# Three scan stages get their first part in the last convolution, and VectorE does the first and the last of the 15 steps of each inverse

## The chip, the cores and the metric

The kernel runs on one core of a Trainium2 chip. Its engines are named as the profile names them: PE (TensorE, matrix products), DVE (VectorE), ACT (ScalarE), POOL (GpSimd), and SP, whose queue issues nearly all of the transfers. Each works through its own instructions in order, and semaphores tie them together. The metric is the device time of one execution, in microseconds (us), as the median of several runs.

## What is computed

One layer of a hybrid model, on 128 context tokens and 2048 latent tokens of 1024 channels. Both token sets are normalised and modulated, go through one input projection, and then through two groups of heads: a delta-rule recurrence (RWKV-7) over 8 heads of 64 channels, run in both directions, and a short gated convolution. An output projection and a last norm follow.

```python
proj = h @ lp['w_in']
r, k, v, g_a, b_gate, c_gate, u_conv, g_b = jnp.split(proj, IN_SPLITS, axis=-1)
...
def step(S, inp):
    r_t, w_t, k_t, v_t, kk_t, a_t = inp
    s_kk = jnp.einsum('bdhij,bdhj->bdhi', S, kk_t)
    S = (S * w_t[..., None, :] - s_kk[..., :, None] * (kk_t * a_t)[..., None, :]
         + v_t[..., :, None] * k_t[..., None, :])
    return S, jnp.einsum('bdhij,bdhj->bdhi', S, r_t)
...
ya = ya.astype(x.dtype) * jax.nn.silu(g_a)
yb = b_gate * _short_conv(c_gate * u_conv, lp['conv_w'], is_latent) * jax.nn.silu(g_b)
u = jnp.concatenate([ya, yb], axis=-1) @ lp['w_out']
return x + gate * u, s_final
```

The recurrence isn't run token by token. The tokens are cut into chunks of 64. In a chunk the corrections of all tokens depend on each other through a triangular matrix of 64 x 64, whose inverse is needed; with it a chunk becomes a few products, and a chain of one small product (S) per chunk carries the state.

## The kernel before

**Three phases.** `phase1` projects the input in three thirds of the tokens. For each third it prepares the recurrence's operands (`recurrence`) and writes them to DRAM, then does the convolution of eight units (`groupB`, four channel groups of two token blocks each); each unit takes 96 matmuls and some DVE and ACT work. `phase2` is the scan: 17 stages, of 16 chunks each (two groups of eight, one per direction). `phase3` is the output projection, whose first parts are mixed into the last stages.

**One stage of the scan** (names as in `SEQ`; a digit at the end is the direction's group):

- *First part.* `L` loads the operands (`rr`). `Gm`, `Qm`, `Fm` are products and transposes on PE (L1019 and L1028); `Ge`, `Fe` (DVE, L1037), `Qe`, `Fa` (ACT) evict them into the stage's slot (`F`, `GA`, `Q`). `dg` (DVE, L1058) takes the diagonal blocks of 32 x 32, `ab` turns them (DVE, L1063), `zi` sets up the inverse `zt` (ACT), `pre` prepares pairs of columns (DVE, L1081 and L1082), and `I` (`inverse`, POOL) does 15 steps of three instructions each: a product into `ztmp` (L1091) and two differences into `zt` (L1094).
- *Second part.* `zr` and `zd` transpose the result (DVE, L1102 and L1105); `U`, `W` (PE), `bu`, `n`, `c0`, `c1` (ACT) join the 32 x 32 blocks to inverses of 64 x 64 in `zb`; `X` (PE, L1171) and `Xc` (ACT) solve; `E` (PE, L1189) and `Ev` (DVE, L1194) build each chunk's operator.
- *The chain.* `S` (PE, L1220) applies the operator to state and values, `sv` (DVE, L1246) scales the new state for the next chunk, `y` collects outputs, and `fw` to `fa` finish a block.

**Order.** `SEQ` is one body of the scan: `S20` is chunk 2 of direction 0 of this stage, `Ge0+3` an eviction of the stage three ahead, `y10+-1` an output of the stage before. So body b works on the chain of stage b, the operators and the inverse's ends of later stages (`I+2`, `zr+2`, `zd+2`, `U+2`), and the first part of stage b + 3. From body 0 on, PE, DVE and ACT keep that order exactly (`manual_schedule`, 13 bodies, then the list `LATE`, which also mixes in `phase3`). POOL, SP and everything ahead of body 0 are put in order by the compiler's own planner, which goes by priority and by which buffers are free; a tile's buffer is free when its last user in the program has run.

**The way in.** While the last third's convolution runs, `early` is stepped four times behind each of its eight units. It opens the right-hand pools of the scan and does the first parts of stages 0 and 1, into two slots in `O.r0`. `main` follows when `phase1` has closed its left-hand pools: `setup_rest` opens `O.l0`, `O.l1` (with `zb`, `zr`, `zd`) and `O.r2` (with the third slot), and the bodies -3 to -1 of `SEQ` fill the pipeline: among them the first part of stage 2 and the second part of stages 0 and 1. `ab` and `zt` have two buffers each, `dg` one.

**Memory.** In `phase1` the raw weight tiles `wr` (two of 4 KB a partition) are in the pool `wp`, beside the split weights `w`, which live to the end of the last convolution. The raw tiles are not used any more in the last third.

Of the kernel before, what the change touches and what calls it, by code (L numbers as in the profile page):

```python
# [6 lines left out]
F32 = mybir.dt.float32  # L7
# [3 lines left out]
ALU = mybir.AluOpType  # L11
# [51 lines left out]
def phase1(K):  # L63
    nc, tc, A, S = K.nc, K.tc, K.A, K.S
    V, G, P, T = nc.vector, nc.gpsimd, nc.scalar, nc.tensor
    cp = Pool(K, "p1c", "left")
    wp = Pool(K, "p1w", "left", 2)
    hl = Pool(K, "p1h", "left", 2)
    tp = Pool(K, "p1t", "left")
    ca = Pool(K, "p1ca", "right")  # L70
    hr = Pool(K, "p1hr", "right")
# [551 lines left out]
    def gate_rows():  # L623
        for b in range(2):
            pr = None
            for k2 in range(4):
                wt = wp.tile([128, 2, 512], F32, tag="wr", name=f"wgate{b}{k2}", bufs=2)
# [45 lines left out]
    for t3, js in enumerate(THIRD):  # L673
# [92 lines left out]
LATE = """  # L766
I@15 sv51@12 fa@10.1 Ge0@16 E110@13 Ev001@13 gh10@14 E010@13 Ev110@13 E100@13 gh00@14 Ev010@13 Gm1@16
# [12 lines left out]
S71@14 CH@4 E110@15 svL1@16 sv71@14 E100@15 CH@5 CD@4 fw@14.0 CD@5 WL@0 zr@16 WL@1 zd@16 U@16 fr@14.0 c1@16  # L780
y11@14 c0@16 Ev100@15 Ev110@15 E111@15 bu@16 E101@15 Ev111@15 WH@0 E000@15 Ev101@15 WH@1 E001@15 WD@0
# [34 lines left out]
def phase2(K):  # L816
# [4 lines left out]
    B = Ctx()  # L821
# [3 lines left out]
    def setup_first():  # L825
# [35 lines left out]
    def setup_rest():  # L861
# [4 lines left out]
        O.r2 = Pool(K, "p2r2", "right")  # L866
        new_slot(O.r2)
        cp = O.l0
# [215 lines left out]
    def inverse(name, s, st, gi):  # L1084

        ab, zt = st.ab, st.zt
        tmp = tl([128, 256], "ztmp", 1, O.rI)
        for m in range(15):
            j, kn, n = 2 * m, m + 1, 30 - 2 * m
# [3 lines left out]
            for r in range(2):  # L1093
                G.tensor_tensor(zt[:, :kn, j + 2:32], zt[:, :kn, j + 2:32], tv[:, :, r], ALU.subtract)  # L1094

    rows = [(slice(sl * 64, sl * 64 + 32), slice(sl * 64 + 32, sl * 64 + 64)) for sl in range(2)]

    def zrows(name, s, st, gi):

        if name == "zr":  # L1100
            st.zr = tl([128, 16, 32], "zr", 1, O.l1)
            V.transpose(st.zr[:].rearrange("p u (q h) -> p q h u", h=2), st.zt[:].rearrange("p q i -> p (q i)"))  # L1102
# [230 lines left out]
    def ending(name, s, st, gi):  # L1333
# [3 lines left out]
        if st.fin is not None:  # L1337
            next(st.fin, None)

    DO = dict(Gm=product, Qm=product, Fm=product, Ge=m_evict, Qe=m_evict, Fa=m_evict, Fe=m_evict, dg=diag, ab=turn, zi=begin, pre=pre, I=inverse,  # L1340
              zr=zrows, zd=zrows, c0=zcopies, c1=zcopies, U=merge, bu=merge, W=merge, n=merge, gh=gcopies, X=solve, Xc=solve,
              E=operator, Ev=operator, S=state, sv=scaled, y=outputs,
              fw=ending, fr=ending, fq=ending, fm=ending, T=ending, fy=ending, fa=ending)
    LOAD = dict(L=load_rr, gsL=load_gs, fsL=load_fs, svL=load_sv)
    SOLO = "ab zi pre I zr zd c0 c1 U bu W n fw fr fq fm T fy fa".split()

# [15 lines left out]
    def first(s):  # L1362
# [23 lines left out]
    def main():  # L1386
# [262 lines left out]
```

## Time and profile before

| what | us |
|---|---|
| median of three runs (1579.95 to 1585.35) | 1580.28 |
| span of the profiled execution, from its first to its last instruction | 1578.3 |
| PE busy | 1499.9 (95%) |
| DVE busy | 1139.9 (72%) |
| ACT busy | 772.3 (49%) |
| POOL busy | 573.8 (36%) |
| POOL, L1094 of the inverse (510 instructions) | 215.4 |
| POOL, L1091 of the inverse (255 instructions) | 139.4 |

The page gives no other time of the profiled execution than its span. The span is cut into places by rows of the timeline: the last third's convolution runs until 946.8 us, the way into the scan follows, the first transposes `zr` of a body are at 988.93 (body 0), 1011.12 (body 1) and so on to 1282.54 (body 12), and the last inverse's `zr` is at 1335.25. An idle time of an engine counts only where another engine waits for what it does next; the page's chain and the waits say where that is.

### The profile page before, as it was taken

What the parts mean: (1) busy time and instruction counts of PE and PEld (TensorE: products, weight loads), DVE (VectorE), ACT (ScalarE), POOL (GpSimd) and SP (SyncE); (2) the same over time, 40 slices, a digit from 0 to 9 for tenths busy, and PEclk for the clock granted to TensorE, in tenths of its full rate; (3) what the DMA queues carried; (4) which work ended last, traced back from release to release, by engine and by line L of the source; (5) the groups of instructions that cost most, each with busy time, mean ns of one, the idle gap of its engine ahead of it and who ended that gap; (6) DMA issues with size and microseconds to landing.
All of it is one profiled execution on the core that took longest, in us unless ns stands there. A gap on an engine that the chain in (4) does not pass through costs nothing.

```text
span 1578.3 us, 39371 instructions
## 1 busy us (share of the span) xinstructions
PE 1499.9 (95%) x16208; PEld 1381.2 (88%) x16208; DVE 1139.9 (72%) x1957; ACT 772.3 (49%) x1462; POOL 573.8 (36%) x962
## 2 busy tenths in 40 slices
PE   5999999999999999999999998999999998899998
PEld 2899999999999999899998997888888886678786
DVE  5999995764999735449985428798998997746533
ACT  4566652432555213135551107887878777523222
POOL 0133330001333100013322805888788887212221
PEclk7899999999999999999999998999999999999999
DMA  9669998663878865438887537566676754646442
GB/s 371 213 174 264 269 270 332 223 223 115 225 220 217 233 226 180 145 116 233 261 218 267 194 125 178 150 188 159 194 192 179 193 163 149 180 142 188 151 143 93
DMA packets 204579, 313.78 MB, mean 199 GB/s; under 512 B 58088, under 2 KB 147560, under 8 KB 190320
## 3 DMA queue, kind: packets, MB, share of 16 engines
q1 hardware_dynamic: 168816, 311.13, 63.9%
q10 hardware_dynamic: 35584, 0.14, 1.4%
q8 instruction: 127, 2.08, 0.6%
q14 instruction: 52, 0.43, 0.1%
HBM read 208.05 MB, written 103.17 MB: 197 GB/s over the span
## 4 chain that ended last, share of the span: by engine, by line
PE 65%; DVE 14%; POOL 7%; issue 5%; DMA 5%; ACT 2%; SPq 0%; ACTq 0%; DVEq 0%; POOLq 0%
POOL zt L1094 4%; PE psu L1503 4%; PE psu L1504 4%; PE psu L1505 4%; PE psE L1189 3%; POOL ztmp L1091 3%; PE mmb L182 2%; PE mmb L184 2%; PE mmb L183 2%; PE psS L1220 2%; PE mmc L182 2%; PE mmc L184 2%; PE mmc L183 2%; PE mmu L182 2%; PE mmu L184 2%
## 5 line engine op out<-in xcount | busy, mean ns | idle before, releaser
L1094 POOL TENSOR_TENSOR zt<-zt,ztmp 128x30 f32<-128x30 f32 (+7 forms) x510 | 215.4, 422 | 39.8
L1091 POOL TENSOR_TENSOR ztmp<-ab,zt 128x60 f32<-128x60 f32 (+7 forms) x255 | 139.4, 547 | 66.7 <-DVE ab L1082 47.0
L410 POOL TENSOR_TENSOR sh<-rawl 128x384 f32<-128x384 f32 (+1 forms) x48 | 47.5, 1007 | 210.1 <-ACT rawl L401 210.1
L1220 PE MATMUL psS<-sv,E 128*64 128x64 f32 x2176 | 104.6, 229 | 12.8 <-DVE sv L1246 7.3
L1220 PEld LDWEIGHTS psS<-sv,E 128*64 128x64 f32 x2176 | 82.8, 137 | 37.9 <-issue 16.3
L1194 DVE TENSOR_TENSOR E<-psE,msk 128x512 f32<-128x512 f32 x136 | 90.6, 683 | 20.0 <-PE psE L1189 18.9
L1568 POOL TENSOR_TENSOR z<-z,x 128x512 f32<-128x512 f32 x32 | 42.7, 1337 | 147.6 <-DVE z L1562 85.7
L1175 ACT ACTIVATE stf<-psX 64x512 f32<-64x512 f32 x136 | 80.3, 590 | 13.1 <-PE psX L1171 10.7
L434 POOL TENSOR_TENSOR hsl<-sq,hsh 128x384 fp32r<-128x384 f32 (+1 forms) x24 | 34.1, 1421 | 129.9 <-ACT hsh L429 121.6
L1246 DVE TENSOR_TENSOR sv<-psS,pc 64x128 f32<-64x128 f32 x254 | 63.7, 271 | 22.4 <-PE psS L1220 21.7
L182 PE MATMUL mmg<-h,w 128*128 128x384 f32 (+1 forms) x216 | 70.8, 328 | 0.0
L183 PE MATMUL mmg<-h,w 128*128 128x384 f32 (+1 forms) x216 | 70.7, 327 | 0.0
L184 PE MATMUL mmg<-h,w 128*128 128x384 f32 (+1 forms) x216 | 70.7, 327 | 0.0
L219 POOL TENSOR_TENSOR hslq<-ssq,hshq 128x384 fp32r<-128x384 f32 (+1 forms) x4 | 4.8, 1202 | 174.2 <-ACT hshq L218 109.6
L182 PE MATMUL mmb<-h,w 128*128 128x384 f32 (+1 forms) x192 | 63.9, 333 | 4.0 <-DMA w<-scr_wsp 4.0
L182 PE MATMUL mmv<-h,w 128*128 128x384 f32 (+1 forms) x192 | 63.1, 329 | 0.9 <-DVE sg L524 0.6
L184 PE MATMUL mmc<-h,w 128*128 128x384 f32 (+1 forms) x192 | 62.8, 327 | 1.0 <-DVE w L154 1.0
L184 PE MATMUL mmb<-h,w 128*128 128x384 f32 (+1 forms) x192 | 63.7, 332 | 0.0
L183 PE MATMUL mmb<-h,w 128*128 128x384 f32 (+1 forms) x192 | 63.6, 331 | 0.0
L182 PE MATMUL mmu<-h,w 128*128 128x384 f32 (+1 forms) x192 | 63.0, 328 | 0.2
L182 PE MATMUL mmc<-h,w 128*128 128x384 f32 (+1 forms) x192 | 63.0, 328 | 0.0
L184 PE MATMUL mmu<-h,w 128*128 128x384 f32 (+1 forms) x192 | 62.9, 328 | 0.0
(312 smaller groups left out, 5019.6 us busy)
## 6 DMA issues: line engine op xcount, KB each, us to landing
w<-scr_wsp SPq DMA_DIRECT2D x68, 1024.0 KB, 5.4
scr_wsp<-w SPq DMA_DIRECT2D x34, 1024.0 KB, 6.0
rr<-scr_ops SPq DMA_DIRECT2D x32, 1024.0 KB, 6.7
scr_ops<-xs SPq DMA_DIRECT2D x160, 192.0 KB, 6.5
wr<-in_win SPq DMA_DIRECT2D x34, 512.0 KB, 8.2
x<-in_x SPq DMA_DIRECT2D x17, 512.0 KB, 3.9
wadas<-in_wada SPq DMA_DIRECT2D x8, 1024.0 KB, 13.9
sv<-scr_vt SPq DMA_DIRECT2D x32, 256.0 KB, 4.0
```

Of the source, the lines that this page charges most:

```text
L182: T.matmul(ps[:, :n], w[:, 0, k], hh[:, 0, k, :n], start=k == 0, stop=False)
L183: T.matmul(ps[:, :n], w[:, 0, k], hh[:, 1, k, :n], start=False, stop=False)
L184: T.matmul(ps[:, :n], w[:, 1, k], hh[:, 0, k, :n], start=False, stop=k == 7)
L1091: G.tensor_tensor(tv, ab[:, j:j + 2, j + 2:32].unsqueeze(1).broadcast_to((128, kn, 2, n)), zt[:, :kn, j:j + 2].unsqueeze(3).broadcast_to(( ...
L1094: G.tensor_tensor(zt[:, :kn, j + 2:32], zt[:, :kn, j + 2:32], tv[:, :, r], ALU.subtract)
L1175: P.activation(g.fs[64:128, :, hd, e::2], g.ps["X"][e][hr_].rearrange("p a (b t) -> p b a t", b=2), AF.Copy, scale=-1.0)
L1194: V.tensor_tensor(g.E[n][:, k:k + 2].rearrange("p a b c -> p (a b) c"), pe[:].rearrange("p a b c -> p (a b) c"), B.msk[:, ME[g.d]].unsquee ...
L1220: T.matmul(g.sp[i // 4][r, q, hd, :], g.E[n][:, k, hd, r], g.sv[:, u, hd, :], start=True, stop=True)
L1246: V.tensor_tensor(dst, g.sp[i // 4][0:64, q], B.pc[0:64, d, 2 * p:2 * p + 2, c:c + 1].broadcast_to((64, 2, 64)), ALU.mult)
L1503: T.matmul(ps[:], mh[:, n], hi[:, cs], start=start and n == 0, stop=False)
L1504: T.matmul(ps[:], mh[:, n], lo[:, cs], start=False, stop=False)
L1505: T.matmul(ps[:], ml[:, n], hi[:, cs], start=False, stop=stop and n == 3)
```

## The change

Four edits. First, `early` does the first part of three stages in place of two; the third slot moves from `O.r2` to a pool of its own, `O.r3`, that is opened with the others. Second, to make room for it, the raw weight tiles of `phase1` get a pool of their own, `wrp`, closed when the last third's convolution begins. Third, the inverse on POOL does steps 1 to 13 only. Step 0 becomes `zf` (`first_row`, two DVE instructions behind `pre`), with `dg` as its scratch tile. Step 14 becomes `zl` (`last_columns`, three DVE instructions ahead of `zr`), with the tile of `zr` as its scratch. Fourth, `zf` and `zl` are put into `SEQ`, `LATE` and `first`. Numbers of buffers stay as they were.

```diff
+    wrp = Pool(K, "p1r", "left")
...
-        raw = wp.tile([128, 8, 128], F32, tag="wr", name=f"wr{cb}_{K.u()}", bufs=2)
+        raw = wrp.tile([128, 8, 128], F32, tag="wr", name=f"wr{cb}_{K.u()}", bufs=2)
...
-            for p in (pax, ta_, hr, ca):
+            for p in (pax, wrp, ta_, hr, ca):
...
-S21 L0+4 Fa0+3 Qe0+3 zi+3 sv30 S40 Fe0+3 fm sv21 sv40 Fm1+3 L1+4 X0+1 S50 pre+3 T sv50 Fa1+3 Fe1+3 S31
-S60 sv31 fy Xc00+1 init+1 y00 Xc10+1 X1+1 S41 Xc01+1 sv60 S70 svL0+2 zr+2 sv41 E000+1 sv70 Xc11+1 Ev000+1
+S21 L0+4 Fa0+3 Qe0+3 zi+3 sv30 S40 Fe0+3 fm sv21 sv40 Fm1+3 L1+4 X0+1 S50 pre+3 T sv50 Fa1+3 Fe1+3 zf+3 S31
+S60 sv31 fy Xc00+1 init+1 y00 Xc10+1 X1+1 S41 Xc01+1 sv60 S70 svL0+2 zl+2 zr+2 sv41 E000+1 sv70 Xc11+1 Ev000+1
...
+        O.r3 = Pool(K, "p2r3", "right")
+        new_slot(O.r3)
...
-        new_slot(O.r2)
...
-        for m in range(15):
+        for m in range(1, 14):
...
+    def first_row(name, s, st, gi):
+
+        ab, zt = st.ab, st.zt
+        t_ = st.dg[:, 0]
+        V.tensor_scalar(t_[:, 2:32], ab[:, 1, 2:32], zt[:, 0, 1:2], None, ALU.mult)
+        V.scalar_tensor_tensor(zt[:, 0, 2:32], ab[:, 0, 2:32], B.ph[:, 2:3], t_[:, 2:32], ALU.mult, ALU.subtract)
+
+    def last_columns(name, s, st, gi):
+
+        ab, zt = st.ab, st.zt
+        st.zr = tl([128, 16, 32], "zr", 1, O.l1)
+        for m in range(14, 15):
+            j, kn, n = 2 * m, m + 1, 30 - 2 * m
+            t_ = st.zr[:].rearrange("p u h -> p (u h)")[:, :kn * 2 * n].rearrange("p (q r i) -> p q r i", r=2, i=n)
+            V.tensor_tensor(t_, ab[:, j:j + 2, j + 2:32].unsqueeze(1).broadcast_to((128, kn, 2, n)),
+                            zt[:, :kn, j:j + 2].unsqueeze(3).broadcast_to((128, kn, 2, n)), ALU.mult)
+            for r in range(2):
+                V.tensor_tensor(zt[:, :kn, j + 2:32], zt[:, :kn, j + 2:32], t_[:, :, r], ALU.subtract)
...
-            st.zr = tl([128, 16, 32], "zr", 1, O.l1)
...
-        for k in ("ab", "zi", "pre", "I"):
+        for k in ("ab", "zi", "pre", "zf", "I"):
...
-        for s in range(2):
+        for s in range(3):
```

In `LATE`, `zl@15` and `zl@16` stand ahead of `zr@15` and `zr@16`, `zf@16` ahead of `I@16`, and `zf@15` ahead of `I@15`. The pool `O.r3` is closed where `O.r2` and `O.r1` are.

More of the change, by code (lines that the diff above doesn't have):

```diff
@@ L626, in gate_rows @@
             for k2 in range(4):
-                wt = wp.tile([128, 2, 512], F32, tag="wr", name=f"wgate{b}{k2}", bufs=2)
+                wt = wrp.tile([128, 2, 512], F32, tag="wr", name=f"wgate{b}{k2}", bufs=2)
                 nc.sync.dma_start(wt[:], A["wada"][4 + b][:, k2 * 2:k2 * 2 + 2])
@@ L766 @@
 LATE = """
-I@15 sv51@12 fa@10.1 Ge0@16 E110@13 Ev001@13 gh10@14 E010@13 Ev110@13 E100@13 gh00@14 Ev010@13 Gm1@16
+zf@15 I@15 sv51@12 fa@10.1 Ge0@16 E110@13 Ev001@13 gh10@14 E010@13 Ev110@13 E100@13 gh00@14 Ev010@13 Gm1@16
 fsL0@14 Ev100@13 gh11@14 S00@13 Ge1@16 S61@12 E111@13 c1@14 sv00@13 E011@13 sv61@12 bu@14 dg0@16 S10@13
@@ L771 @@
 X1@14 fm@11.0 Xc00@14 ab@16 S50@13 S21@13 Xc10@14 T@11.0 Xc01@14 E000@14 sv50@13 sv21@13 S60@13 Ev000@14
-E010@14 zi@16 Xc11@14 sv60@13 S31@13 Ev010@14 S70@13 E100@14 svL0@15 sv70@13 sv31@13 pre@16 I@16 E110@14 Ev100@14
+E010@14 zi@16 Xc11@14 sv60@13 S31@13 Ev010@14 S70@13 E100@14 svL0@15 sv70@13 sv31@13 pre@16 zf@16 I@16 E110@14 Ev100@14
 fy@11.0 E001@14 fsL0@15 gsL0@15 gh00@15 Ev110@14 S00@14 Fm1@16 gh10@15 sv00@14 fa@11.0 S10@14 E011@14
 fw@11.1 Fa1@16 y01@13 sv10@14 y10@13 Ev011@14 S41@13 S20@14 y00@13 sv41@13 E111@14 sv20@14 Ev001@14
-S51@13 S30@14 sv51@13 E101@14 sv30@14 zr@15 S61@13 fsL1@15 gsL1@15 gh01@15 S40@14 sv40@14 U@15 sv61@13 zd@15
+S51@13 S30@14 sv51@13 E101@14 sv30@14 zl@15 zr@15 S61@13 fsL1@15 gsL1@15 gh01@15 S40@14 sv40@14 U@15 sv61@13 zd@15
 gh11@15 S50@14 fr@11.1 S71@13 svL1@15 c0@15 sv50@14 sv71@13 S60@14 Ev111@14 c1@15 sv60@14 Ev101@14 S70@14
@@ L779 @@
 sv31@14 fa@11.1 y11@13 X1@15 y00@14 S41@14 Xc01@15 sv41@14 y01@14 S51@14 Xc11@15 sv51@14 S61@14 sv61@14
-S71@14 CH@4 E110@15 svL1@16 sv71@14 E100@15 CH@5 CD@4 fw@14.0 CD@5 WL@0 zr@16 WL@1 zd@16 U@16 fr@14.0 c1@16
+S71@14 CH@4 E110@15 svL1@16 sv71@14 E100@15 CH@5 CD@4 fw@14.0 CD@5 WL@0 zl@16 zr@16 WL@1 zd@16 U@16 fr@14.0 c1@16
 y11@14 c0@16 Ev100@15 Ev110@15 E111@15 bu@16 E101@15 Ev111@15 WH@0 E000@15 Ev101@15 WH@1 E001@15 WD@0
@@ L1338, in ending @@
             next(st.fin, None)
-    DO = dict(Gm=product, Qm=product, Fm=product, Ge=m_evict, Qe=m_evict, Fa=m_evict, Fe=m_evict, dg=diag, ab=turn, zi=begin, pre=pre, I=inverse,
+    DO = dict(Gm=product, Qm=product, Fm=product, Ge=m_evict, Qe=m_evict, Fa=m_evict, Fe=m_evict, dg=diag, ab=turn, zi=begin, pre=pre, I=inverse, zf=first_row, zl=last_columns,
               zr=zrows, zd=zrows, c0=zcopies, c1=zcopies, U=merge, bu=merge, W=merge, n=merge, gh=gcopies, X=solve, Xc=solve,
@@ L1344, in phase2 @@
     LOAD = dict(L=load_rr, gsL=load_gs, fsL=load_fs, svL=load_sv)
-    SOLO = "ab zi pre I zr zd c0 c1 U bu W n fw fr fq fm T fy fa".split()
+    SOLO = "ab zi pre zf I zl zr zd c0 c1 U bu W n fw fr fq fm T fy fa".split()
     def do(name, s):
@@ L1401, in main @@
                 O.r2.close()
+                O.r3.close()
                 O.r1.close()
```

## The prediction

> **What bounds the kernel now.** I read the page first, to find which engine is named. Then I read the stretches of the scan, the waits inside them, and the rows of the places that the change touches. The chain that ended last:
>
> ```profile
> PE 65%; DVE 14%; POOL 7%; issue 5%; DMA 5%; ACT 2%; SPq 0%; ACTq 0%; DVEq 0%; POOLq 0%
> ```
>
> TensorE carries two thirds of it and POOL 7%, all of that in L1091 and L1094, the inverse. POOL's share alone would make the inverse a good target. The stretches show how close the engines stand (start:end, length, then busy time of PE, PEld, DVE, ACT, POOL, the granted clock, DMA share and GB/s): the last convolution, the way into the scan, and twelve bodies of the scan.
>
> ```profile
> 832.60:946.80 114.20, 114.17 (x972) 111.21 (x974) 47.00 (x95) 12.70 (x32) 41.23 (x90) 0.98 0.55 191
> 946.80:965.00 18.20, 13.62 (x327) 12.50 (x328) 16.65 (x33) 15.48 (x31) 3.15 (x8) 0.72 0.87 200
> 986.50:1282.50 296.00, 280.25 (x7150) 247.23 (x7144) 267.05 (x540) 236.01 (x450) 250.61 (x540) 0.99 0.66 181
> ```
>
> In the convolution PE is busy for all but 0.03 us, so whatever PE work is added there lengthens it. On the way into the scan DVE is busiest, 16.65 of 18.2 us. In the twelve bodies (296.0 / 12 = 24.67 us each) PE is busy 280.25, DVE 267.05 and POOL 250.61 us. POOL looks free for 45 us, but its 45 small instructions of a stage leave gaps, so rows must say whether it is late. These are waits between 986 and 1283 us, as who waits for whom: us, times, longest.
>
> ```profile
> DVE GA L1037 <- PE psGm L1019: 10.9, 9, 4.3
> PE psS L1220 <- DVE sv L1246: 4.6, 15, 0.4
> PE psS L1220 <- DVE E L1194: 1.8, 6, 0.5
> DVE zr L1102 <- POOL zt L1094: 1.1, 3, 0.7
> ```
>
> The last row decides much. The only consumer of a finished inverse is the transpose `zr`, and it waited for POOL three times, 1.1 us in all. The chain walks along POOL for a long way because POOL itself never pauses, yet the other engines are only 1.1 us ahead of it over twelve bodies. PE, by contrast, waits 4.6 + 1.8 = 6.4 us for DVE.
>
> **The change part by part.** 1. *POOL loses two of fifteen steps a stage.* The groups of instructions with those steps' shapes, from 986.5 to 1282.5 us (twelve stages):
>
> ```profile
> L1094 POOL TENSOR_TENSOR zt<-zt,ztmp 128x30 f32<-128x30 f32 x48 | 13.6, 284 | 3.8
> L1091 POOL TENSOR_TENSOR ztmp<-ab,zt 128x60 f32<-128x60 f32 x24 | 8.7, 363 | 5.0 <-DVE ab L1082 3.2
> ```
>
> That is (13.6 + 8.7) / 12 = 1.86 us of work, and with gaps of (3.8 + 5.0 - 3.2) / 12 = 0.47 us, 2.3 us a stage. What it can give back is the wait that it causes: 1.1 us at most while the other engines stay as they are. **Term: -1.1 us.**
>
> 2. *DVE gains five small instructions a stage.* Nothing in the trace has their exact shapes, so their neighbours bound them:
>
> ```profile
> L98 DVE TENSOR_SCALAR dv<-vec 128x12 f32<-128x12 f32 x2 | 0.3, 168 | 0.0
> L98 DVE TENSOR_SCALAR ov<-pv,dv 128x64 f32<-128x64 f32 x2 | 0.5, 247 | 0.0
> L614 DVE SCALAR_TENSOR_TENSOR ov<-pv,dv,ov 128x64 f32<-128x64 f32 x2 | 0.6, 278 | 0.0
> L286 DVE TENSOR_TENSOR sh<-psmod,vec 128x8 f32<-128x8 f32 x2 | 0.3, 160 | 1.1 <-PE psmod L280 1.1
> L593 DVE TENSOR_TENSOR sh<-ob,mmb 128x128 f32<-128x128 f32 x2 | 0.6, 280 | 0.0
> ```
>
> `first_row` is a tensor_scalar and a scalar_tensor_tensor of 30 elements: between 168 and 247 ns, and between 160 and 278 ns; I take 0.20 + 0.21 = 0.4 us. `last_columns` is a product of 60 and two differences of 30 elements, each between 160 and 280 ns: 0.21 + 0.18 + 0.18 = 0.6 us. So 1.0 us a stage (0.8 to 1.3), 12 us over the twelve bodies. They cost nothing as far as they fall into DVE's idle 296.0 - 267.05 = 28.95 us. They cost their full time where PE stands waiting for DVE already. Both happen. A body's last microseconds on PE, with the idle time in brackets:
>
> ```profile
> 1230.81 0.45 PE L1220 MATMUL psS<-sv,E 128*64 128x64 f32 x8 [0.43 <-DVE sv L1246]
> 1233.36 0.45 PE L1220 MATMUL psS<-sv,E 128*64 128x64 f32 x8 [0.42 <-DVE sv L1246]
> ```
>
> Both waits lie just behind the place where `zf` is put into DVE's order: behind `zf` are queued `sv31`, `y` and `sv60`, and S on PE waits for those `sv`. So `zf` mostly passes on to PE. Behind `zl` are queued `zr`, `sv41` and `zd`; PE's U waits for `zr` and S for `sv41`, but E stands between and gives cover. And 10.9 us of DVE's idle time is one wait, for Gm, which runs on PE behind U, that is behind `zr`: a later `zr` doesn't shorten it. I therefore take half, 6 us. **Term: +6.0 us**, bounds 0 (all in idle time) and +15.6 (1.3 us, twelve times, all passed on).
>
> 3. *The first part of stage 2 moves into the convolution.* Its PE work there, by what stages 0 and 1 paid (chain of waits, start, us, what):
>
> ```profile
> 846.47 1.03 PE psGm L1019 x32
> 847.50 0.32 PE mmgb L182
> ...
> 853.23 0.18 PE mmc L182
> ...
> 855.31 0.44 PE psQm L1028 x4
> ...
> 859.84 1.03 PE psFm L1019 x32
> ```
>
> Two Gm, two Qm and two Fm make 2 x (1.03 + 0.44 + 1.03) = 5.0 us. The first convolution matmul after each of them took 0.32 instead of 0.18, six times 0.14 = 0.8. PE has no cover there. **Term: +5.8 us.** Its evictions go to DVE and ACT, busy 47.0 and 12.7 of 114.2 us, and cost nothing. The loads of `rr` stand in SP's queue beside the `w` loads as those of stage 1 do; if one of them waits there for Fm with a `w` load behind it, PE would starve, and I hold up to 3 us for that in the range.
>
> What goes from behind the convolution:
>
> ```profile
> 946.87 0.95 POOL L907 MEMSET zb<- 128x1024 f32 x1 [40.76 <-PE mmb L184]
> 950.77 1.03 DVE L1102 STREAM_TRANSPOSE zr<-zt 128x512 f32<-128x512 f32 x1
> 953.77 2.47 DVE L1037 TENSOR_TENSOR GA<-psGm,mkg 128x512 f32<-128x512 f32 x4
> 951.85 1.20 PE L1119 MATMUL psU<-zr,GA 32*32 32x32 f32 x64 [3.13 <-DVE gwh L872]
> 954.50 2.89 PE L1019 MATMUL psFm<-rr 64*64 64x128 f32 x32 [1.45 <-DVE GA L1037]
> 957.32 1.97 PE L1028 MATMUL psQm<-idt,rr 128*128 128x128 f32 x8
> 957.05 0.79 DVE L1058 SCALAR_TENSOR_TENSOR dg<-GA,hm 128x256 f32<-128x256 f32 x2
> 957.88 2.08 DVE L1063 STREAM_TRANSPOSE ab<-dg 128x1024 f32<-128x1024 f32 x1
> 957.47 1.18 ACT L1122 COPY zd<-psU 32x512 f32<-32x512 f32 x2
> 961.08 2.09 PE L1019 MATMUL psFm<-rr 64*64 64x128 f32 x30
> 962.34 0.29 POOL L1091 TENSOR_TENSOR ztmp<-ab,zt 128x60 f32<-128x60 f32 x1 [14.51 <-DVE ab L1082]
> 963.50 0.76 DVE L1037 TENSOR_TENSOR F<-psFm,msk 128x256 f32<-128x256 f32 x2 [0.69 <-ACT F L1051]
> ```
>
> PE sheds 2.89 + 1.97 + 2.09 = 6.95 us, more than it costs in the convolution. But PE is not what is late: it idled 3.13 us before U, which needs `zr` from DVE, and W behind it needs ACT's copy that ends at 958.65, while Qm ends at 959.29. Taken alone that frees 0.6 us. DVE, the busiest, sheds the four GA evictions (2.47), two `dg` (0.79) and four F evictions (two pairs at 0.76): 4.8 us, and takes up two `zl` and a `zf`, 1.6 us. I take DVE's net, 3.2 us, as the gain, since its row is the fullest; bounds 0.6 and 6.95. **Term: -3.2 us.**
>
> The *inverse* of stage 2 doesn't come along, and so this is where the change may not do what its name says. `ab` and `zt` keep two buffers each. Stage 2 needs those of stage 0, which are free once `zl` and `zr` of stage 0 have read them, and these write `st.zr` in the pool of `zb`: the memset of `zb`, in the same pool, waited for the last convolution matmul until 946.87. So turn, begin, pre, `zf` and the inverse of stage 2 still come behind it. POOL gets no stage ahead.
>
> 4. *The end of the scan.* `zl` of the last stage lies on the chain:
>
> ```profile
> 1335.33 0.97 DVE zr L1102
> ```
>
> 0.6 us for that, and half of `zl` of stage 15 and of two `zf` (1.4 us): **term +1.3 us.** Moving the raw weight tiles to a pool of their own changes no instruction of the first phase: nothing.
>
> Sum: -1.1 + 6.0 + 5.8 - 3.2 + 1.3 = +8.8 us. The profiled execution spans 1578.3 us; the median of the three runs, 1580.28, lies 2.0 us above that span. 1578.3 + 8.8 = 1587.1 of span, and 1589.1 with the 2.0.
>
> **The rivals.** (a) *POOL was the pace after all.* If POOL's 2.3 us a stage come off the five stages in which the chain runs along it (1157 to 1282 us), and DVE's work falls into its waits for POOL and PE, the loop loses 11.5 us: -11.5 + 5.8 - 3.2 + 1.3 = -7.6, so 1572.7; PE's own 280.25 us set the floor, -15.75 in place of -11.5, 1568.4. For it: the chain. Against: `zr` waited 1.1 us. It decides if DVE's waits for PE shrink as much as POOL does. (b) *DVE's idle time takes everything up*: -1.1 + 5.8 - 3.2 = +1.5 and 0.6 for the last `zl`, 1582.4. For it: 28.95 us of idle time for 12 us of work. Against: 21 waits of PE for DVE. (c) *Everything is passed on*: +12 instead of +6 and +0.8 more at the end, 1595.9. For it: PE and DVE stand at 95% and 90%, with an order fixed by hand.
>
> (d) *The slow clock behind the convolution lasts longer.* The granted clock there (same columns as the stretches above):
>
> ```profile
> 949.00:952.00 3.00, 0.15 (x9) 0.15 (x10) 2.97 (x9) 2.48 (x6) 0.00 (x0) 1.00 0.73 185
> 954.00:962.00 8.00, 7.50 (x122) 6.74 (x126) 7.97 (x12) 7.18 (x15) 0.00 (x0) 0.50 1.04 216
> 964.00:967.00 3.00, 2.58 (x64) 1.90 (x56) 0.26 (x1) 2.52 (x5) 2.45 (x8) 1.00 1.05 378
> ```
>
> After a pause of some 3 us PE ran at half clock, and was back at full clock by 964, after 8 us in which it was busy 7.50. Fm and Qm were that work. Without them PE has only U, W and X to run, with pauses, and may stay at half clock into the E products: the 2.58 us of 964 to 967 and as much behind them would take twice as long, +5 us, 1594.1. [...] (e) *The inverse of stage 2 does run in the convolution*: its turn of 2.08 us (row of `ab`) leaves DVE's way too, 1587.0.
>
> **How the numbers follow.** Forecast 0.35, with a range of its own of 1585 to 1594; (b) 0.28; (c) 0.14; (d) 0.08; (a) 0.12; (e) 0.03. A measurement can tell about 0.5% from no change, here 7.9 us: 1572.4 and 1588.2. Faster: two thirds of (a) and 0.04 for startup and clock falling better than their bounds, 0.12. Within: (b), (e), a third of (a), and somewhat under half of the forecast, 0.50. Slower: the rest, 0.38. The range, 1573 to 1599, leaves out most of (a), and the end of (c) and (d) added up.
>
> **What would show it.** Right: the last convolution some 6 us longer in the PE rows, with Gm, Qm and Fm of a third stage in it; the first POOL instruction of the third inverse still behind the last convolution matmul; DVE's wait for POOL at `zr` gone and POOL pausing before each inverse; bodies of about 25 us, with PE's waits for `sv` grown from 4.6 to some 10 us. Wrong: a body near 23.5 us would show (a), an unchanged 24.6 (b), 25.7 (c); a third inverse before the convolution ends would show (e); a clock of 0.5 beyond 20 us behind the convolution would show (d).

## The result, and the profile after

The changed kernel took 1594.93 us (median of 4, 1592.65 to 1599.69) against 1580.38 for the kernel before (median of 4, 1579.95 to 1585.35): a ratio of 1.0087, with a 95% interval of 1.0066 to 1.0108. It is slower by 14.5 us; 1589.1 had been forecast. The profiled execution took 1596.06 us and spans 1594.2, against 1578.3 before. The chain that ended last, from the page of the changed kernel:

```profile
PE 66%; DVE 19%; DMA 6%; issue 5%; ACT 3%; SPq 1%; ACTq 0%; POOL 0%; DVEq 0%; POOLq 0%
```

POOL went from 7% to 0% and DVE from 14% to 19%. The inverse is off the chain, and the time has become longer all the same. The stretches of the changed kernel (columns as in the prediction): from a product of the convolution ahead of the first of stage 2 to the convolution's end, the pause behind it, U to the first E, and the twelve bodies.

```profile
858.70:950.80 92.10, 91.57 (x847) 87.97 (x845) 39.02 (x83) 10.87 (x28) 33.93 (x72) 1.00 0.48 171
950.80:960.60 9.80, 0.04 (x3) 0.06 (x3) 9.62 (x23) 6.69 (x13) 0.95 (x1) 0.76 0.78 167
960.60:976.40 15.80, 13.06 (x274) 12.16 (x276) 3.87 (x10) 10.44 (x19) 11.10 (x25) 0.50 0.55 101
995.00:1291.00 296.00, 278.30 (x7110) 244.23 (x7112) 278.33 (x604) 235.12 (x447) 227.25 (x472) 1.00 0.65 181
```

In the second row PE did nothing for 9.8 us while DVE was busy for 9.62. In the third PE was busy for 13.06 of 15.8 us, all of it at half clock, a granted 0.50. In the bodies DVE went from 267.05 to 278.33 us and POOL from 250.61 to 227.25.

**The convolution.** The products of stage 2 in it (timeline of PE: start, us, what):

```profile
889.07 1.10 PE L1021 MATMUL psGm<-rr 64*64 64x128 f32 x32
...
894.73 1.11 PE L1021 MATMUL psGm<-rr 64*64 64x128 f32 x32 [0.53 <-DMA rr<-scr_ops]
...
899.70 1.03 PE L1030 MATMUL psQm<-idt,rr 128*128 128x128 f32 x8
...
908.64 1.10 PE L1021 MATMUL psFm<-rr 64*64 64x128 f32 x32
...
912.86 1.10 PE L1021 MATMUL psFm<-rr 64*64 64x128 f32 x32
```

That is 5.44 us of work and one wait of 0.53 for `rr`. From one and the same product of the convolution, ahead of these (at 861.09 us before, at 858.68 after), to the convolution's end it took 85.72 us before and 92.13 after, 6.4 more. (The end itself, 946.81 and 950.81, shows only 4.0 more, because the first phase ahead of that product happened to be 2.4 us shorter in this execution.)

**The way into the scan.** DVE's timeline of the changed kernel behind the convolution:

```profile
951.78 1.41 DVE L918 COPY stf<-I 64x512 f32<-64x512 f32 x4
953.13 1.42 DVE L918 COPY stg<-I 64x512 f32<-64x512 f32 x4
954.47 1.41 DVE L918 COPY sth<-I 64x512 f32<-64x512 f32 x4
955.81 0.20 DVE L1112 TENSOR_TENSOR zr<-ab,zt 128x60 f32<-128x60 f32 x1
956.04 2.05 DVE L1065 STREAM_TRANSPOSE ab<-dg 128x1024 f32<-128x1024 f32 x1
957.88 0.27 DVE L1115 TENSOR_TENSOR zt<-zt,zr 128x30 f32<-128x30 f32 x1
958.13 1.12 DVE L1083 TENSOR_TENSOR dg<-ab 128x512 f32<-128x512 f32 x1
959.17 0.19 DVE L1115 TENSOR_TENSOR zt<-zt,zr 128x30 f32<-128x30 f32 x1
959.39 1.04 DVE L1122 STREAM_TRANSPOSE zr<-zt 128x512 f32<-128x512 f32 x1
```

The first `zr` starts 8.6 us behind the convolution; before it was 4.0 (950.77). Two things stand ahead of it that did not before: the presets of `sth`, and, between the three instructions of `zl`, stage 2's turn and half of its `pre`. Here the planner has put other work that was ready between instructions that depend on each other, and the first instruction of `zl` is what frees the buffer that the turn needs. What PE did then, in the changed kernel:

```profile
960.58 1.92 PE L1139 MATMUL psU<-zr,GA 32*32 32x32 f32 x64 [9.77 <-DVE zr L1122]
...
968.50 5.87 PE L1191 MATMUL psX<-F,zb 64*64 64x128 f32 x64 [0.43 <-ACT zb L1150]
974.30 1.97 PE L1209 MATMUL psE<-stg,stf 128*64 128x128 f32 x16
```

and X in the kernel before, which stood right behind Fm of stage 2:

```profile
963.05 2.35 PE L1171 MATMUL psX<-F,zb 64*64 64x128 f32 x62
```

The same product takes 5.87 us in place of 2.35. The half clock lasted from 955.8 to 976.3 us by the trace's clock record, 20.5 us; before it was 10.2.

The inverse of stage 2 starts behind the convolution, as forecast (POOL's timeline):

```profile
963.42 0.38 POOL L1093 TENSOR_TENSOR ztmp<-ab,zt 128x112 f32<-128x112 f32 x1 [11.60 <-DVE zt L1115]
```

**The twelve bodies.** Waits from 995 to 1291 us (who for whom: us, times, longest), and the new DVE instructions by shape in the same stretch:

```profile
PE psS L1240 <- DVE sv L1266: 9.3, 22, 0.7
DVE GA L1039 <- PE psGm L1021: 5.6, 9, 1.1
PE psS L1240 <- DVE E L1214: 2.1, 6, 0.5
PE psS L1240 <- DVE sg L1341: 1.5, 5, 0.3
```
```profile
L1115 DVE TENSOR_TENSOR zt<-zt,zr 128x30 f32<-128x30 f32 x26 | 6.3, 241 | 0.9
L1103 DVE SCALAR_TENSOR_TENSOR zt<-ab,ph,dg 128x30 f32<-128x30 f32 x13 | 3.3, 251 | 0.5
L1102 DVE TENSOR_SCALAR dg<-ab,zt 128x30 f32<-128x30 f32 x13 | 3.0, 232 | 0.0
L1112 DVE TENSOR_TENSOR zr<-ab,zt 128x60 f32<-128x60 f32 x13 | 2.9, 220 | 0.0
```

A stage pays 0.23 + 0.25 + 0.22 + 2 x 0.24 = 1.18 us on DVE. PE's waits for DVE are 9.3 + 2.1 + 1.5 = 12.9 us, and were 6.4. Yet the twelve bodies, from `zr` of body 0 to `zr` of body 12, took 293.97 us against 293.60: something else fell (below, at "More work for DVE in the loop").

### The profile page after: what moved, and what is told of

It reads as the page before. It is cut to its first block, busy times and chain, and to the rows that moved or that the text cites. A ratio compares the mean times of both kernels' runs of the same rounds, so it can differ in the third digit from the quotient of the medians.

```text
span 1594.2 us, 39360 instructions
## 1 busy us (share of the span) xinstructions
PE 1503.3 (94%) x16208; PEld 1382.5 (87%) x16208; DVE 1156.2 (73%) x2042; ACT 772.3 (48%) x1462; POOL 531.9 (33%) x860
## 4 chain that ended last, share of the span: by engine, by line
PE 66%; DVE 19%; DMA 6%; issue 5%; ACT 3%; SPq 1%; ACTq 0%; POOL 0%; DVEq 0%; POOLq 0%
PE psE L1209 5%; PE psu L1524 4%; PE psu L1525 4%; PE psu L1526 4%; PE psS L1240 2%; PE mmb L183 2%; PE mmb L184 2%; PE mmb L185 2%; DVE E L1214 2%; PE mmc L183 2%; PE mmc L185 2%; PE mmu L185 2%; PE mmgb L185 2%; PE mmu L184 2%; PE mmgb L184 2%
## 5 line engine op out<-in xcount | busy, mean ns | idle before, releaser
L1096 POOL TENSOR_TENSOR zt<-zt,ztmp 128x56 f32<-128x56 f32 (+6 forms) x442 | 188.6, 427 | 34.6
L1093 POOL TENSOR_TENSOR ztmp<-ab,zt 128x112 f32<-128x112 f32 (+6 forms) x221 | 127.0, 575 | 107.0 <-DVE zt L1103 57.2
L1240 PE MATMUL psS<-sv,E 128*64 128x64 f32 x2176 | 104.8, 229 | 18.0 <-DVE sv L1266 12.4
L1214 DVE TENSOR_TENSOR E<-psE,msk 128x512 f32<-128x512 f32 x136 | 90.5, 681 | 21.6 <-PE psE L1209 20.9
L1266 DVE TENSOR_TENSOR sv<-psS,pc 64x128 f32<-64x128 f32 x254 | 63.4, 270 | 21.9 <-PE psS L1240 21.2
L183 PE MATMUL mmb<-h,w 128*128 128x384 f32 (+1 forms) x192 | 62.8, 327 | 2.7 <-DMA w<-scr_wsp 2.7
L185 PE MATMUL mmk<-h,w 128*128 128x384 f32 (+1 forms) x184 | 60.3, 328 | 2.6 <-DVE w L155 2.6
L185 PE MATMUL mmb<-h,w 128*128 128x384 f32 (+1 forms) x192 | 62.7, 327 | 0.0
```

Source lines behind the costliest of these rows:

```text
L183: T.matmul(ps[:, :n], w[:, 0, k], hh[:, 0, k, :n], start=k == 0, stop=False)
L185: T.matmul(ps[:, :n], w[:, 1, k], hh[:, 0, k, :n], start=False, stop=k == 7)
L1093: G.tensor_tensor(tv, ab[:, j:j + 2, j + 2:32].unsqueeze(1).broadcast_to((128, kn, 2, n)), zt[:, :kn, j:j + 2].unsqueeze(3).broadcast_to(( ...
L1214: V.tensor_tensor(g.E[n][:, k:k + 2].rearrange("p a b c -> p (a b) c"), pe[:].rearrange("p a b c -> p (a b) c"), B.msk[:, ME[g.d]].unsquee ...
L1240: T.matmul(g.sp[i // 4][r, q, hd, :], g.E[n][:, k, hd, r], g.sv[:, u, hd, :], start=True, stop=True)
```

## The experiments

What the profiles of the experiments show is put beside the two first profiles in one table. Its columns: from the same product of the convolution as above to the convolution's end; from there to U and to X; from X to the first E; from there to `zr` of body 0; the length of the half clock in that place; the twelve bodies; from `zr` of body 12 to that of the last stage. All in us, each of one execution.

| kernel | conv. | to U | to X | X to E | E to zr | half clock | bodies | end | ratio to before (95%) |
|---|---|---|---|---|---|---|---|---|---|
| before | 85.72 | 5.04 | 16.03 | 2.81 | 23.3 | 10.2 | 293.6 | 52.7 | 1 |
| r1_before | 85.72 | 5.05 | 16.03 | 2.86 | 21.9 | 10.2 | 295.0 | 55.2 | - |
| after | 92.13 | 9.77 | 17.69 | 5.80 | 23.0 | 20.5 | 294.0 | 59.3 | 1.0087 (1.0066 to 1.0108) |
| r1_after | 92.72 | 9.77 | 17.69 | 5.80 | 27.4 | 30.7 | 297.2 | 53.2 | 1.0077 (1.0047 to 1.0108) |
| e1_first_part_only | 92.26 | 6.17 | 14.67 | 5.67 | 22.9 | 17.1 | 297.3 | 54.1 | 1.0086 (1.0056 to 1.0116) |
| e2_steps_only | 85.72 | 5.75 | 16.52 | 2.57 | 24.9 | 13.7 | 298.9 | 55.5 | 1.0040 (1.0020 to 1.0060) |
| e4_presets_pool | 91.55 | 7.07 | 14.99 | 5.80 | 26.5 | 27.3 | 296.2 | 56.0 | 1.0092 (1.0064 to 1.0121) |
| e5_zf_twice | 92.09 | 9.75 | 17.68 | 5.76 | 24.9 | 20.5 | 299.4 | 57.1 | 1.0118 (1.0090 to 1.0145) |
| e9_after_warm | 91.93 | 15.38 | 21.04 | 6.23 | 26.9 | 20.5 | 299.4 | 54.8 | 1.0117 (1.0089 to 1.0146) |
| e11_after_filled | 92.11 | 9.76 | 17.03 | 5.77 | 23.2 | 6.8 | 296.6 | 54.6 | 1.0123 (1.0100 to 1.0145) |
| e12_only_gm_early | 88.59 | 10.14 | 18.27 | 5.80 | 28.1 | 27.3 | 295.1 | 55.0 | 1.0088 (1.0067 to 1.0108) |
| e13_zr_first | 93.04 | 2.82 | 15.57 | 5.26 | 23.3 | 17.1 | 291.4 | 55.2 | 1.0071 (1.0042 to 1.0100) |
| e6_before_presets_pool | 85.72 | 1.54 | 19.24 | 5.80 | 21.8 | 20.5 | 295.7 | 51.8 | 1.0048 (1.0027 to 1.0068) |
| e10_before_warm | 85.73 | 6.32 | 19.06 | 4.70 | 20.9 | 10.2 | 295.5 | 52.7 | 1.0024 (0.9999 to 1.0049) |

An interval of a ratio is some 3 to 5 us to each side. So a part of 2 or 3 us is read from the stretches, and the ratios bear out only the sums.

The column of the bodies needs care. Spells of half clock come inside the bodies too, in kernels of both kinds. In the fourteen profiles, each of the eight bodies that take over 27 us (of 168) has such a spell in it: two in e1, one each in before, e2, e4, e6, e9 and e10. The median body, which a spell doesn't move, is the same in both kernels: 24.3 and 24.6 us in the two profiles of before, 24.6 and 24.3 in those of the changed kernel. It is 25.1 in e5 and 24.2 to 24.8 in all the others. What brings such spells on was not tested.

### Both kernels once more

> The kernel before, unchanged, for a second profile. Theory A: what differs from the first profile at unchanged work (waits for weights in the first phase, the half-clock spell of 6.8 us at 830.6 us, the 2.8 us issue stall of U at 1090) comes and goes by execution; the stretches that the change touches (first third-stage product in the convolution to its end; its end to the first bodies) repeat within 1 us. Rival: the stalls on PE sit at fixed instructions and repeat, and so belong to the code's layout.

> The changed kernel, unchanged, on the chip of the other kernels here. If the loss of 0.87% is the change's: ratio 1.007 to 1.011 to the kernel before again. In the profile the convolution takes 6 to 7 us longer from 870 us on, the way into the scan 4 to 5, and the half clock behind the convolution lasts about 20 us as in the first profile (20.5), if that is no accident of one execution.

The loss repeats: 1600.59 us against 1586.84, a ratio of 1.0077, and spans of 1601.3 and 1587.0. The expected 4 to 5 us on the way into the scan and the 20 us of half clock do not: they were 10.1 and 30.7. The second pair, after less before, by stretch: first phase -5.4, convolution +7.0, way into the scan +10.1, bodies +2.3, end -2.1, rest +2.4; together 14.3. The first pair: -2.4, +6.4, +4.4, +0.4, +6.6, +0.5; together 15.9. The convolution's loss and U, X and E behind it repeat within 0.6 us. The first phase and the end do not: they vary by 2.5 to 6.1 us from one execution of the same kernel to the next. Nor did the 2.83 us stall of U at 1090 come back in r1_before. One stall stands at the same instruction of both kernels, with varying length (the first row is of r1_before, the second of after):

```profile
1292.58 0.25 PE L1119 MATMUL psU<-zr,GA 32*32 32x32 f32 x3 [1.66 <-issue]
```
```profile
1296.30 0.25 PE L1139 MATMUL psU<-zr,GA 32*32 32x32 f32 x3 [2.24 <-issue]
```

It was 0.56 in the first profile of before. So the +6.6 at the end of the first pair is mostly not the change's. The first phase varies alike with and without the raw weight tiles' own pool: that product starts at 861.1 to 867.6 us in the five kernels without it (mean 864.3) and at 858.7 to 868.1 in the nine with it (mean 864.2). That edit costs nothing, as forecast.

In r1_after the half clock lasted 30.7 us. From 971.7 us on PE had no pause, and yet the half clock ended only at 988.4, 16.7 us later (r1_after, most of that stretch):

```profile
971.70:988.00 16.30, 16.30 (x161) 14.65 (x163) 3.51 (x8) 11.16 (x19) 13.08 (x29) 0.50 0.01 4
```

### The first part alone, and the steps alone

e1: the changed kernel with 15 steps on POOL and without `zf` and `zl` (also out of `SEQ` and `LATE`). e2: the kernel before with `zf` and `zl`, with two early stages (and the pools as before).

```diff
# e1, against after
-        for m in range(1, 14):
+        for m in range(15):
...
-        for k in ("ab", "zi", "pre", "zf", "I"):
+        for k in ("ab", "zi", "pre", "I"):
...
```

```diff
# e2, against after
-        for s in range(3):
+        for s in range(2):
...
```

> Edits one and two alone: three stages get their first part in the last convolution, POOL does all 15 steps again, no zf, no zl. Theory A (the loss sits on the way into the scan: DVE's planned order puts the first zr late, PE stands idle, then runs at half clock): the last convolution still ends about 4 us later (about 950.9 us), zr of body 0 stands behind the twelve preset copies, its idle time before U is 5 to 8 us, zr of body 0 comes at 994 to 998 (988.9 before, 997.3 after); the bodies have no added DVE work, so the total is 1585 to 1590. Theory B (the added DVE instructions in the loop are what costs): this kernel loses only the convolution's 4 us and gains DVE's net on the way in, so 1580 to 1583.

> Edits three and four alone: VectorE does the first and the last step of each inverse; two stages get their first part in the convolution, as before. Theory A: the last convolution ends at about 946.9 as before; zl of stage 0 delays the first zr by about 0.9 us only, so zr of body 0 comes at 989 to 991; the bodies are some 0 to 4 us longer in all; total 1580 to 1584. Theory B: about +6 us over twelve bodies and +2 to +6 at the end; total 1586 to 1592. In both, DVE's wait for POOL at zr is gone.

The totals in these texts count from 1580.4 us; in this set of runs the kernel before took 1585.53. Against that e1 (1599.32) lost 13.8 us, more than the 5 to 10 of theory A and far more than B gave it, and e2 (1591.91) lost 6.4, at the lower end of B's. By stretches e1 lost 6.5 us in the convolution and 1.2 to 2.5 on the way into the scan (43.3 against 42.1 and 40.8). That is 8 to 9 us, which is where its interval begins (1.0056 is 8.9). Its profile shows one thing more: 13.6 us of half clock inside the bodies, the most of all, with bodies of 29.1 and 27.6 us; its median body is 24.5. In e2 the way into the scan is 1.9 to 3.2 us longer and the bodies 3.9 to 5.3, but two bodies (27.8, with 6.8 us of half clock, and 27.0) account for that, and the median body is 24.4. So these single profiles do not show that the new DVE instructions themselves lengthen the bodies. The two losses, 13.8 and 6.4 us, add up to more than the changed kernel's 13.8; with intervals of 3 to 5 us to each side that can be noise. What does follow the new instructions is PE's waits for DVE in the bodies: e1 has those of the kernel before, and e2 those of the changed kernel (e1, then e2):

```profile
PE psS L1241 <- DVE sv L1267: 5.6, 15, 1.7
PE psS L1241 <- DVE E L1215: 1.4, 4, 0.5
```
```profile
PE psS L1239 <- DVE sv L1265: 9.9, 24, 0.8
PE psS L1239 <- DVE E L1213: 1.6, 4, 0.5
PE psS L1239 <- DVE sg L1340: 1.4, 5, 0.3
```

So 7.0 us without the new DVE instructions and 12.9 with them. This sum was 6.4 and 7.5 in the two profiles of before, 12.9 and 11.9 in those of after, 13.3 in e13. In the other kernels it was 5.1 and 7.1 without these instructions (e6, e10) and 11.5 to 13.3 with them (e4, e9, e11, e12), so it tells the two kinds apart in every profile.

### More work for DVE in the loop

```diff
# e5, against after: both instructions of zf
+        for _ in range(2 if s > 2 else 1):
```

> The changed kernel with both instructions of zf issued twice for stages 3 to 16 (the second time they write the same values): 14 times about 0.45 us more DVE work in the loop, 6 us in all. If all of it is passed on to PE: +6 us over the changed kernel, about 1601. If half is, as the prediction took: +3, about 1598. If DVE's idle time absorbs it: within 1 us of 1594.9. PE's waits for sv in the twelve bodies (9.2 us in the changed kernel) should grow by what is passed on.

The groups of e5 show 0.240 + 0.250 us for the two instructions, so 5.9 us more in twelve bodies. PE's waits for DVE in e5:

```profile
PE psS L1242 <- DVE sv L1268: 13.5, 33, 0.8
PE psS L1242 <- DVE sg L1343: 4.3, 5, 0.9
PE psS L1242 <- DVE E L1216: 2.2, 6, 0.5
```

They come to 20.0 us, 7.6 more than the mean of the two profiles of after (12.4). All of the added work is passed on to PE's waits, and not half; for `sv` alone it is 4.2 us against the first profile of after (13.5 and 9.3). The bodies took 299.4 us, 5.4 and 2.1 more than in the two profiles of after. The total rose by 4.4 us by the medians (1604.97 against 1600.59) and by 6.5 by the ratios (1.0118 against 1.0077), which have their own sets of runs of the kernel before. With intervals of some 5 us the totals do not tell all from half.

What falls in return are PE's pauses for which the profile shows no releaser ("issue"). Summed over the same bodies they are 8.8 and 9.2 us in the kernel before, 6.4 in e1, 4.8 in e2, 3.6 and 5.8 in the changed kernel, 2.5 in e5 and 0.7 in e13. The more PE waits for DVE, the shorter are these pauses, so that the two together range from 13.4 to 17.7 us in all of these but e5 (22.5). Why they fall, no run tested. DVE's own wait for Gm fell too, from 10.9 and 8.3 us in the two profiles of before to 5.6 and 7.6 in those of after.

### The presets on POOL

```diff
# e4, against after; e6: the same against before
-            V.tensor_copy(t_[0:64, 0, hd], B.I2[0:64].unsqueeze(1).broadcast_to((64, 8, 64)))
+            G.tensor_copy(t_[0:64, 0, hd], B.I2[0:64].unsqueeze(1).broadcast_to((64, 8, 64)))
```

> The changed kernel with the preset copies of the scan's state tiles on POOL in place of DVE: the same values, written by another engine. Theory A: the first zr comes 3 to 5 us earlier behind the convolution, PE's idle time before U shrinks from 9.8 to 5 to 7 us, full clock returns earlier, and zr of body 0 comes 3 to 8 us earlier than 997.3; total 1587 to 1592, against 1594.9 of the changed kernel. Rival: the order of the first zr decides nothing, since DVE's other work there (turn, pre, evictions) is what is late; total within 2 us of the changed kernel.

> The kernel before with the preset copies of the scan's state tiles on POOL in place of DVE, as a candidate that beats both kernels. If the first zr is what PE waits for on the way into the scan: zr 2 to 3 us earlier behind the convolution, ratio 0.998 to 0.999. Rival, as the same edit in the changed kernel gave no gain: within 2 us, ratio 0.999 to 1.002.

In e4 the first `zr` came 5.9 us behind the convolution in place of 8.6, and X at 15.0 in place of 17.7. The total did not follow (1600.67 against 1600.59): X still took its 5.8 us, and the half clock lasted 27.3 us, so that with 47.3 us to body 0 it stood between the two profiles of the changed kernel (46.5 and 50.9). In e6 the first `zr` came after 0.4 us, and the kernel was slower by 0.48%: X stood 3.2 us later than before and at half clock. An earlier first `zr` alone gained nothing in either kernel. (The profile of e6 is of the fastest of its twelve executions, 1588.72 us, with a median of 1592.93.)

### Filling PE's pauses

```diff
# e9 (18 products, after) and e10 (6, before), behind setup_rest()
+        K.body = -3
+        warm = O.pm.tile([128, 512], F32, tag="m", name="warm")
+        for _ in range(18):
+            T.matmul(warm[:], B.idt[:], B.slots[0][0][1][:, 0:4].rearrange("p a c -> p (a c)"), start=True, stop=True)
```

> The changed kernel with 18 products of 128x512 behind the last convolution, into a tile that nobody reads, so that PE doesn't idle before U. If the half clock of some 20 us (955.9 to 976.4) is due to that pause and costs PE's work there double time: no half clock in 951 to 976, X takes 2.4 in place of 5.9 us and the first E 1.1 in place of 2.0, the bodies begin 4 to 6 us earlier, total 4 to 6 us below the changed kernel. Rival: DVE's queue is what is late there, and a faster PE only waits longer: less than 1.5 us.

> The kernel before with 6 such products behind the last convolution. If the half clock of 10 us there costs time: 2 to 4 us below the kernel before (953.4 to 963.6 us at half clock with 7.5 us of PE work). Rival: DVE is late there, not PE, and the six products are in the way: 0 to 2 us slower.

The size was a miss. The 18 products took 15.6 us, and U came 5.6 us late; in e10 the six took 5.2. But in e9 a half clock of 20.5 us came all the same, only later, from 975.0 us on, when PE had U, W and short pauses; in e10 it was 10.2 us, from 961.6 on, and lay over X. e11 has the filling at its right size, 11 products behind the convolution and 3 between U and W:

> The changed kernel with 11 products of 128x512 (0.87 us each at full clock, from the kernel with 18) behind the last convolution and 3 between U and W of stage 0, so that PE is busy in the pauses of 9.8 and 2.3 us and U isn't put off. If the half clock on the way into the scan comes from those pauses and is what costs there: full clock in the stretch, X 2.4 in place of 5.9 us, zr of body 0 at 41 to 43 us behind the end of the convolution (46.5 and 50.8 in the two profiles of the changed kernel, 42.1 and 40.7 in those of the kernel before), total 4 to 8 us below the changed kernel, ratio about 1.004 to 1.006. Rival: DVE's and ACT's work there sets the pace; zr of body 0 stays at 46 us or more, ratio 1.008 to 1.010.

Stretches of e11: the pause, U and W, and X.

```profile
953.70:963.40 9.70, 9.40 (x22) 3.80 (x20) 9.57 (x23) 6.61 (x12) 0.95 (x1) 1.00 0.76 175
963.40:970.70 7.30, 6.26 (x200) 4.33 (x200) 3.67 (x9) 5.29 (x11) 3.73 (x10) 1.00 1.10 203
970.70:976.50 5.80, 5.59 (x66) 4.92 (x66) 0.11 (x1) 3.24 (x6) 5.02 (x11) 0.58 0.03 8
```

U was on time and at full clock, and so was W. X was not: the half clock began at 971.6, behind 2.3 us of U and W in blocks of 32x32 and a pause of 0.68, and lasted 6.8 us, just over X. So X to E stays at 5.8 us. Body 0 came 46.0 us behind the convolution, near the better profile of the changed kernel (46.5), and the total was no smaller: the ratio of 1.0123 is the largest of all. Why, the profile can't show, since it is of the fastest of the six executions (1596.59 us, with a median of 1604.55). The experiment shortened the half clock to a third, but did not take it from X, so what X would take at full clock in the changed kernel was not tried.

### Leaving Qm and Fm behind the convolution

```diff
# e12, against after
-        for kinds in (("Gm", "Ge", "dg"), ("Qm", "Qe"), ("Fm", "Fa", "Fe")):
+        for kinds in (("Gm", "Ge", "dg"), ("Qm", "Qe"), ("Fm", "Fa", "Fe"))[:1 if s == 2 else 3]:
...
-        for k in ("ab", "zi", "pre", "zf", "I"):
+        for k in ("ab", "zi", "pre", "zf", "I") if s < 2 else ():
```

So turn to `zf` of stage 2 are left to `SEQ` too.

> The changed kernel with only the Gm part (Gm, Ge, dg) of stage 2 in the last convolution; Qm, Fm and their evictions stay behind it, as in the kernel before. If PE work added to the convolution passes on in full and Qm and Fm are what keeps PE's clock up behind it: the convolution grows by 2 to 3 us in place of 6.4 to 7.0, the half clock behind it lasts about 10 us, zr of body 0 comes 42 to 45 us behind the convolution; total 6 to 9 us below the changed kernel, ratio 1.002 to 1.005. Rival: the late first zr (presets, turn and pre stand ahead of it) decides: 46 us or more, ratio 1.006 to 1.008.

The convolution grew by 2.9 us in place of 6.4, so PE's work there is passed on in full. Behind it, though, Qm and Fm ran at once, ahead of a pause of 7.3 us before U, and the half clock lasted 27.3 us, with X at 5.8. In the kernel before and in e2 Fm stood right ahead of X, without a pause to X, and X to E took 2.6 to 2.9 us. So the amount of PE work behind the convolution does not decide by itself. With Fm right ahead of X the spell was 10.2 us in all four profiles (before, r1_before, e2, e10; e2 has 3.4 us more, from 977.1 on). Where Fm ran ahead of a pause (e6, e12) or in the convolution, it was 17.1 to 30.7, except for e11's 6.8. This doesn't make X fast in every case: in e10 the spell began later and lay over X, which took 4.7 us to E.

### The first zr first

```diff
# e13, against after: DVE keeps this order up to body 0
+        for k in ("zl", "zr", "zd"):
+            do(k, 0)
...
+        with tc.manual_schedule(engines={mybir.EngineType.DVE}):
+            setup_rest()
```

Turn to `zf` of stage 2 are left to `SEQ` here, as in the kernel before.

> The changed kernel with zl, zr and zd of stage 0 written as DVE's first instructions behind the last convolution, ahead of the twelve presets and of turn and pre of stage 2; all edits of the change stay. If the late first zr is the cause of the longer way into the scan: zr of stage 0 some 2 us behind the convolution in place of 8.5, PE's pause before U about 3 us in place of 9.8, zr of body 0 at 41 to 45 us behind the end of the convolution in place of 46.5 and 50.8, and the total 3 to 7 us below the changed kernel, ratio 1.003 to 1.006. Rival: what follows U (ACT's copies, the half clock, zr of stage 1 behind presets, turn and pre) sets the end of this stretch, whatever the first zr does: 46 us or more, ratio 1.007 to 1.010.

PE in e13:

```profile
964.00 1.92 PE L1142 MATMUL psU<-zr,GA 32*32 32x32 f32 x64 [2.82 <-DVE zr L1125]
972.17 0.28 PE L1150 MATMUL psW<-zb,zd 32*32 32x32 f32 x2 [6.26 <-issue]
```

U came after 2.8 us in place of 9.8. Then the wait moved: 6.26 us before W. The profile names no releaser for it ("issue"), but W reads `zd`, which ACT's `bu` writes. ACT's first instruction behind the convolution, and `bu`:

```profile
961.21 0.62 ACT L1183 COPY stg<-GA 64x512 f32<-64x512 f32 x1 [2.49 <-PE mmb L185]
...
971.50 1.18 ACT L1145 COPY zd<-psU 32x512 f32<-32x512 f32 x2
```

Between them ACT had no pause: the copies into `stg` and `sth`, `zi` of stage 2 and `c0` stand ahead of `bu`. X came 2.1 us earlier than in the changed kernel and body 0 after 44.2 us, between the two kernels as expected. The total, a ratio of 1.0071, is not to be told from the changed kernel's 1.0077 and 1.0087.

No version here beats the kernel before: e6 and e10, the two that start from it, are slower by 0.48% and, if at all, by 0.24%.

## Why the prediction was right in its direction, and where it was wrong

- **The direction and the range held, in part by luck.** 1594.9 lies within 1573 to 1599, 5.8 us above the forecast; the range is 26 us wide, and the narrower one given for the forecast's own mechanism, 1585 to 1594, just misses it. No change within 0.5% had been given 0.50, and slower than that, which came, 0.38. The sum of the terms was +8.8; the two pairs of profiles give +15.9 and +14.3. The luck is that errors of opposite sign met: the way into the scan was forecast 7.6 to 13.3 us too low, the loop 2.6 to 4.5 us too high.
- **The convolution, forecast +5.8: right.** It measured +6.4 and +7.0, and +2.9 with Gm alone. The products took 1.10 rather than 1.03 us, and one waited 0.53 for `rr`.
- **The way into the scan, forecast -3.2: wrong, and this is the step that failed.** It measured +4.4 and +10.1. The prediction took "DVE's net, 3.2 us, as the gain, since its row is the fullest". But the four GA evictions that DVE shed stood *behind* the first `zr`; nothing ahead of it became shorter, and `zl`, the `sth` presets, a turn and half a `pre` came in front. X came 1.7 us later instead of earlier. The rest is rival (d): X to E took 3.0 us more at half clock, and behind E it was -0.3 in one execution and +5.5 in the other, where the half clock lasted 30.7 us. The rival's sign came true, a clock of 0.5 beyond 20 us behind the convolution: it ended 25.5 and 34.4 us behind it. It had been priced at +5, 1594.1 in all, and was given a chance of 0.08. That its time is the nearest of all owes something to the same luck.
- **DVE's new work in the bodies, forecast +6.0: right for the waits, wrong for the time.** PE's waits for DVE grew by 5.5 us (mean 12.4 against 7.0). A stage's work was 1.18 us, not 1.0; and e5 shows that `zf`, which stands right ahead of `sv`, is passed on whole to these waits. But the bodies took only 0.4 and 2.3 us longer, against +4.9 with POOL's term: 24.5 and 24.8 us each, where about 25 had been forecast. The forecast lacked what fell in return: some 4 us of issue pauses, and some 3 of DVE's wait for Gm, of which the prediction had said that "a later `zr` doesn't shorten it".
- **POOL's relief, forecast -1.1: right as far as it can be read.** DVE's wait for POOL at `zr` is gone from the waits, and POOL pauses before inverses (45.1 us before the first step in twelve bodies). The bodies did not become shorter, which refutes rival (a).
- **The end, forecast +1.3**: +6.6 and -2.1. The two differ by more than the term, so it is left open.
- **Rivals (b), (c), (e).** The sign of (b), a body of an unchanged 24.6 us, is closer to what came than the forecast's own, but not by its mechanism, since PE's waits did grow; its total, 1582.4, lacks the way into the scan. (c) gave 1595.9, near the result, but its bodies of 25.7 us did not come. (e) is refuted by POOL's row at 963.42.

So the loss lies in the convolution and on the way into the scan, and hardly in the loop. The 5.8 us that the forecast lacked are what is left of the error on the way in, after the loop's error of the other sign.

What stays open: why the half clock lasted 17 to 31 us in kernels whose PE was at work, how much of the way in's loss it makes, when such spells come in the bodies, and what e1 and e2 lose beyond the stretches ahead of the bodies.

## What to carry to other kernels

Work that is taken from a busy engine shortens a stretch only if it stood ahead of the instruction that the next engine waits for (here 2.47 us of GA evictions left DVE's queue behind the first `zr`, and X came 1.7 us later): read the order in the queue first, and the busy time after it. PE work moved into a stretch where PE is busy throughout costs its full time there (here 6.4 us, for 5.4 of products and a wait of 0.5), and its old place may have needed it: with Fm right ahead of X the half clock lasted 10.2 us, without it mostly 17 to 31. A longer wait in the profile is not yet a longer stretch: here 5.5 us more of waits came with 0.4 and 2.3 us more of time. Where single executions differ by several us, compare stretches between the same instructions of two executions of each kernel, and a sum of waits that repeats.

## What the runs showed of the hardware that was not expected

- **The half clock outlasted a full load.** In r1_after PE was busy for all of 16.30 us at a granted clock of 0.50, and for 7.70 of 7.70 from 968.5 to 976.2 in the first profile of after. On the way into the scan it lasted 6.8 to 30.7 us in all, and under X, E and Gm products without a pause (in r1_after the first S products too) it went on for 7.8 and 16.7 us. The products' own times agree with the clock record: in the first profile of after 16 E products took 1.97 us at 974.3, at a clock of 0.50, and 1.04 at 982.1, at 1.00.
- **PE paused where the profile shows nothing that it waited for.** In some 294 us of the scan of the kernel before these pauses came to 8.8 and 9.2 us, single ones up to 2.83, and they fell to 0.7 to 5.8 us in kernels in which PE waited more for DVE.
- **Half clock came inside a busy scan too.** PE was busy for 278.0 of the 293.6 us of the bodies in the kernel before; a spell of 3.4 us at 0.50 began at 1090.1, right behind a pause of 2.83, in a body that took 27.35 us where the median is 24.3.
- **The tiny DVE instructions took 0.22 to 0.25 us each** (30 or 60 elements a partition): five of them came to 1.18 us, half of what the POOL steps they replace took in the kernel before (2.3 us with gaps).
